# Start addresses of the on-chip tiles that TensorE reads, moved to multiples of 256 bytes

## The chip, the cores and the metric

The kernel runs on one core of a Trainium2 chip. The metric is device time in microseconds of one execution; the time given for a kernel is the median over runs. A core has a matrix engine (TensorE, PE in the profile, with its weight loads listed apart as PEld), three engines for elementwise work (VectorE = DVE, ScalarE = ACT, GpSimd = POOL), and SyncE (SP), which here only issues transfers. On-chip memory has 128 partitions; a tile takes the same range of bytes in each of them, and "address" below means the byte at which that range begins.

## What is computed

A decoder trunk of two layers over 1024 tokens with 1024 channels, batch 1, all in float32. Cut to what matters:

```python
def reference(x, ...):
    h = x
    for layer in range(2):
        n = rms_norm(h, norm1_g[layer])
        if layer % 2 == 0:
            mix = retention_rwkv_mixer(n, ...)   # 8 retention heads and 8 RWKV-7 heads, one output projection
        else:
            mix = swa_sink_mixer(n, ...)         # 16-head sliding-window attention (128) with sinks
        h = h + mix
        n = rms_norm(h, norm2_g[layer])
        h = h + (silu(n @ w_gate) * (n @ w_up)) @ w_down    # 2816 hidden channels
    return rms_norm(h, final_g)
```

## The kernel before

Activations are held transposed: channels on partitions, tokens along the tile, in two halves of 512 tokens. Every large product is made of matmuls with a 128x128 piece of weights held in the array (the stationary operand) and a 128x512 piece of activations streaming through it (the moving operand). To keep float32 accuracy with the faster fp32r format, each operand x is kept as a pair, hi = x rounded to fp32r and lo = x - hi, and each product is three matmuls: hi with hi, weights hi with activations lo, weights lo with activations hi. Those three are the lines 345 to 347 in `gemm`, 1168 to 1170 in `prod`, and three calls of line 239 (`mm`) in the first mixer's planner.

The order of stages, with the profile's times: the first mixer up to about 660 us (projections interleaved with many small float32 matmuls of the RWKV and retention heads; a planner with costs and due times written by hand sets that order); its output projection up to about 730; the FFN of layer 0 up to about 1345; attention up to about 1780; the FFN of layer 1 up to about 2340; the last norm. The FFNs use a two-by-two Strassen-like scheme with seven products instead of eight. `ffn_early` makes two of the products for each pair of hidden tiles; `late` (called by `ffn_pair`, eleven pairs a layer) makes the other five for the gate and the up matrix in step. Of these five, two have moving operands in `n8` tiles (`X["t2"]`, `X["t1"]`) and three in `cb` tiles (`X["t3"]`, `X["t4"]`, `X["22"]`). `down` and `rest_d` make the down projection, with moving operands in `n8` and `ha`.

Weights arrive by DMA in `wr`, `wq` or `wd` tiles and are split into hi and lo by ACT and by POOL or DVE into a tile of 128x1024 that holds 4 pieces of each (`wsplit`, lines 330 and 331; `vsplit`, lines 1341 and 1342). These tiles come from `wtile`: four buffers `w` in the pool `pp`, in some stages also the two `wr` buffers, and around attention two buffers `wx` in the pool `at`, one after the other in turn. `attn` projects with 12 weight tiles a half, `w_o` with 8.

Where tiles lie: a pool takes its memory from the left end or from the right end (`side`). Within a pool, tiles lie one behind the other in the order in which their tags first come. `t` rounds a tile up to a multiple of 16 words, 64 bytes. On the left stand 1024 bytes of scratch for DMA descriptors (line 1823), four small constants of 32 bytes each, and then `pp`, which stays open for the whole run: `pv` (98 words, rounded to 448 bytes), `c_ones` (512), `c_eps` (64), `wr`, `w`, `c_ident`, `n8`, `nq`. The pools opened later on the left (`rp`, `hx`, `nb`, `sp` of layer 1, `ft`, `wqa`, `wqb`, `fa`, `fz`) begin where `pp` ends. On the right stands a `pad` of 480 bytes, and the others stack down from it: `mx` (held as `mp`) and `mz` in the first mixer, later `hy`, `sp` of layer 0, `cb`, `nB`, `at`. Addresses in the first mixer, before the change:

```
pp:  pv 1152   c_ones 1600   c_eps 2112   wr 2176, 6272   w 10368 ...   c_ident 26752   n8 27264 ...
rp:  r2 68224 ...   c_cos, c_sin 84608, 86656   z 88704   c_dmask 90816   c_qdec 91840   rvm 92352   Sc 92416
mz:  rr 94272   rkk 98368   rv 102464   BK 107072
mp:  hv 119360   hk 119424   zlast 119488   Srw 119552   ...   id2 126848   gup 127104   ...   vm 219520   X 219648
```

When a pool is opened where another one stood, each new tile waits until the old tiles that it overlaps have been read for the last time (`reuse_waits="tile"`).

Every address used in this text is the one that the program's allocation gives for the named tile; the trace itself holds no addresses.

Of the kernel before, what the change touches and what calls it, by code (L numbers as in the profile page):

```python
# [10 lines left out]
F32 = mybir.dt.float32  # L11
# [5 lines left out]
P = 128  # L17
T = 1024
HT = 512
# [185 lines left out]
class Kern:  # L205
    def __init__(self, ctx, tc, A, out):
        self.ctx, self.tc, self.nc, self.A, self.out = ctx, tc, tc.nc, A, out
        nc = self.nc
        self.pp = ctx.enter_context(tc.tile_pool(name="pp", bufs=1, side="left"))
        self.dr = ctx.enter_context(tc.tile_pool(name="dr", bufs=2, space=bass.MemoryType.DRAM))  # L210
        self.n = 0
        pad = ctx.enter_context(tc.tile_pool(name="pad", bufs=1, side="right"))
        pt = pad.tile([P, 120], F32, tag="pad", name="pad")
        nc.gpsimd.memset(pt, 0.0)
        nc.scalar.activation(pt[:, :16], pt[:, :16], AF.Copy)
        self.pv = self.t(self.pp, [P, NPV], "pv")
        nc.scalar.dma_start(self.pv, A["pvec"])
        self.cst = {}
        for nm in ("ones", "eps"):
            self.cst[nm] = self.const(self.pp, nm)  # L220
        self.h, self.plan = [None, None], None
        self.wx = None
        self.w6, self.nw, self.owed, self.lo = False, 0, [], self.nc.gpsimd
        self.hid = [self.dram(f"hid{i}", [FT, P, HT]) for i in range(4)]
        self.hc = [self.dram(f"hc{L}", [NP, 4, P, 2, HT]) for L in range(2)]
        self.bd = self.dram("bd", [KT, P, HT])
        self.u0d = self.dram("u0", [NP, 2, P, HT])
        self.wsp = self.dr.tile([30, 2, P, 2, HT], F32, tag="wsp", name="wsp", bufs=1)
        self.cats = [self.dram(f"cat{hf}", [KT, P, HT]) for hf in range(2)]
# [37 lines left out]
    def t(self, pool, shape, tag, bufs=1, dt=F32):  # L267

        self.n += 1
        n = math.prod(shape[1:])  # L270
        if n % 16 == 0:
            return pool.tile(shape, dt, tag=tag, name=f"{tag}_{self.n}", bufs=bufs)
        t = pool.tile([shape[0], -(-n // 16) * 16], dt, tag=tag, name=f"{tag}_{self.n}", bufs=bufs)[:, :n]
        return t.rearrange("p (a b) -> p a b", b=shape[2]) if len(shape) == 3 else t

    def n8(self, pool):

        return [self.t(pool, [P, 2, HT], "n8", 8, F32R) for _ in range(8)]
# [112 lines left out]
    def mixer0(self):  # L391
        nc = self.nc
        gm, mp = self.pool("mx", "right")
        gz, self.mz = self.pool("mz", "right")
        gr, rp = self.pool("rp", "left")
        self.mp, self.rp = mp, rp
        hv = self.t(mp, [P, 12], "hv")
        nc.vector.tensor_scalar(
            out=hv[:, 0:8], in0=self.pv[:, PV["w0"] : PV["w0"] + 8], scalar1=0.5, scalar2=None, op0=ALU.mult
        )  # L400
        hk = self.t(mp, [P, 8], "hk")
        ka = self.pv[:, PV["ka"] : PV["ka"] + 4]
        nc.vector.tensor_scalar(out=hk[:, 0:4], in0=ka, scalar1=0.5, scalar2=None, op0=ALU.mult)
        nc.vector.tensor_scalar(out=hk[:, 4:8], in0=ka, scalar1=-0.5, scalar2=1.0, op0=ALU.mult, op1=ALU.add)
        self.hv, self.hk = hv, hk
        self.zlast = self.t(mp, [P, 14], "zlast")
        nc.gpsimd.memset(self.zlast, 0.0)
        self.Srw = self.t(mp, [P, 4, 64], "Srw")
        self.Sret = self.t(mp, [P, 4, 64], "Sret")
        self.wa, self.gl, self.cs, self.rs = None, None, None, None  # L410
        nc.gpsimd.memset(self.Srw, 0.0)
        nc.gpsimd.memset(self.Sret, 0.0)
        pl = self.plan = Plan(self)
        pq = self.psum("ps0", {"f": 3, "m": 4, "c": 1})
        self.pr, self.st, self.rst, self.dns, self.nds, self.last = {}, {}, {}, {}, {}, {}
        units = [(0, 0), (0, 2), (1, 0), (1, 2)]

        def jobs(hf, what, ps):
            for p in ps:
                if what == "rkv":  # L420
                    for i, nm in enumerate("rkv"):
                        self.shifted(hf, 4 * i + p, nm, p)
                else:
                    self.ret_jobs(hf, p)


        pl.chain(self.first_norm())
        for u, (hf, p0) in enumerate(units):
            pl.chain(self.unit(u, hf, (p0, p0 + 1)))
        for u, (hf, p0) in enumerate(units):  # L430
            for p in (p0, p0 + 1):
                pl.chain(self.pair(u, hf, p))
        for hf in range(2):
            for p in range(4):
                pl.chain(self.ret(hf, p))
        pl.chain(self.second_norm())
        self.lora(0)
        jobs(0, "rkv", (0, 1))
        jobs(0, "ret", (0, 1))
        jobs(0, "rkv", (2, 3))  # L440
        jobs(0, "ret", (2, 3))
        self.lora(1)
        jobs(1, "rkv", (0, 1))
        jobs(1, "ret", (0,))
        jobs(1, "rkv", (2, 3))
        jobs(1, "ret", (1, 2, 3))
        self.lo = nc.vector
        pl.run()
        self.lo = nc.gpsimd
        gr.__exit__(None, None, None)  # L450
        self.ghx, self.hx = self.pool("hx", "left")
        self.h[0] = self.wout(0, self.heads(0, self.n8(self.pp)), self.s8(self.hx, "h0", 2))
        gz.__exit__(None, None, None)
        gb, nb = self.pool("nb", "left")
        ch = self.heads(1, self.n8(nb), self.last)
        gm.__exit__(None, None, None)
        return pq, gb, nb, ch
# [27 lines left out]
    def loads(self):  # L485

        nc, mp, rp = self.nc, self.mp, self.rp
        x0 = []
        first = [self.plan.jobs[i] for i in range(4)]

        self.plan.twice = [j["col"] for j in first[:3]]
        for k in range(KT):
            x = self.t(rp, [P, HT], "r2", 8)
            self.keep(nc.sync.dma_start(x, self.A["xT"][k, :, 0:HT]))
            x0.append(x)
            if k == 0:
                raw = self.t(self.pp, [P, 1024], "wr", 2)
                for o in (0, HT):
                    self.keep(nc.sync.dma_start(raw[:, o : o + HT], self.A["w_in"][first[0]["col"]][:, o : o + HT]))
                first[0]["hl"] = self.wsplit(raw)  # L500
            if k == 4:
                raw = self.t(self.pp, [P, 1024], "wr", 2)
                self.keep(nc.sync.dma_start(raw, self.A["w_in"][first[1]["col"]]))
                first[1]["hl"] = self.wsplit(raw)
        for j in first[2:]:
            raw = j["raw"] = self.t(self.pp, [P, 1024], "wr", 2)
            self.keep(nc.sync.dma_start(raw, self.A["w_in"][j["col"]]))
        wua = self.t(mp, [P, 512], "wua")
        self.keep(nc.sync.dma_start(wua[0:64, :], self.A["w_up"]))
        self.keep(nc.sync.dma_start(wua[64:128, :], self.A["a_up"]))  # L510
        for nm in ("blk", "smask", "gmask", "ident", "kdec", "gam", "id2"):
            self.cst[nm] = self.const(self.pp if nm == "ident" else mp, nm, eng=nc.sync)
        gup = self.t(mp, [P, 512], "gup")
        nc.sync.dma_start(gup, self.A["g_up"])
        self.wua, self.gup = wua, gup
        return x0
# [99 lines left out]
    def shifted(self, hf, ti, nm, p):  # L616
# [3 lines left out]
        def evac(ps):  # L620
            tag = {"r": "rr", "k": "rkk", "v": "rv", "w": "wa", "g": "gl"}[nm]
            t = self.t(self.mz if nm in "rkv" else self.mp, [P, (64 if nm == "v" else 0) + HT], tag, 1 if nm == "w" else 2)
            out = t[:, 64:] if nm == "v" else t
            z = self.t(self.rp, [P, HT + 1], "z", 1)
            nc.gpsimd.tensor_copy(z[:, 0:1], self.zlast[:, ti : ti + 1])
            nc.vector.tensor_tensor(out=z[:, 1 : HT + 1], in0=ps, in1=self.rs, op=ALU.mult)
            nc.gpsimd.tensor_copy(self.zlast[:, ti : ti + 1], z[:, HT : HT + 1])
# [20 lines left out]
    def pair(self, u, hf, p):  # L648


        nc, mp = self.nc, self.mp
# [120 lines left out]
        for w in range(2):  # L772
            ps = self.pst("m", [P, 4, 2, 64])
            for j in range(4):
                o = 64 * (1 - w) + 128 * j
                self.tr(ps[:, j].rearrange("p e t -> p (e t)"), vp[:, o : o + 128], ident)
            mean = self.t(mp, [P, 4, 2], "vm", 2)
            V.tensor_reduce(out=mean, in_=ps, axis=AX.X, op=ALU.add, negate=True)

            if w == 0:  # L780
# [24 lines left out]
        for c in range(NCH):  # L805
            for e in range(2):
                b = half[1 - e]
# [211 lines left out]
    def ret(self, hf, p):  # L1019
        nc, mp = self.nc, self.rp  # L1020
# [18 lines left out]
        ps = self.pst("m", [P, 8, 64])  # L1039
        for c in range(4):  # L1040
            self.tr(ps[:, 2 * c : 2 * c + 2, :].rearrange("p e t -> p (e t)"), v[:, P * c : P * c + P], ident)
        mean = self.t(mp, [P, 8], "rvm", 1)
        V.tensor_reduce(out=mean, in_=ps, axis=AX.X, op=ALU.add, negate=True)
        vt = self.t(mp, [P, 4, 2, 64], "r2", 8)
        V.scalar_tensor_tensor(
# [788 lines left out]
```

## Time and profile before

| | us |
|---|---|
| median of 3 runs | 2386.26 (2385.11 to 2391.5) |
| span of the profiled execution | 2386.7 |
| PE busy, share of the span | 2323.7, 97% |
| weight loads (PEld), inside PE's time | 1829.0, 77% |
| DVE, ACT, POOL busy | 1669.3, 1053.3, 949.0 |
| mean granted TensorE clock | 0.990 of full |
| mean busy share of the 16 DMA engines | 0.49 |

The span is the time from the first to the last instruction of one profiled execution. Matmuls are pipelined: one starts while its predecessor is still draining, so the durations in the profile (390 ns and more for a 128x512 fp32r matmul) are longer than the spacing of the starts, and it is the spacing that adds up to the time. It is read from the timeline, which has a row per matmul in order of time, as the difference of two start times divided by the number of rows between them.

### The profile page before, as it was taken

To read this page: it belongs to the slowest core of one execution; us is meant where nothing else is said; L and a number is where in the kernel's file an instruction comes from. 1 tells how busy PE (TensorE), PEld (TensorE's weight loads), DVE (VectorE), ACT (ScalarE), POOL (GpSimd) and SP (SyncE) were. 2 spreads that over 40 slices of the span, in tenths; PEclk is the share of its full clock that TensorE was granted. 3 is DMA by queue.
4 is the path that set the end of the run, shared out by engine and by line. 5 is a ranking of instruction groups with operands and counts; after the bars stand their busy time and mean duration, and the time that the engine had idled before them with its cause. 6 is when DMAs were issued, how large, how long until landed. Compare 5 with 4: busy or idle time off the path is not lost. (4 is left out here: it accounts for less than half of the span.)

```text
span 2386.7 us, 35626 instructions
## 1 busy us (share of the span) xinstructions
PE 2323.7 (97%) x13092; PEld 1829.0 (77%) x13092; DVE 1669.3 (70%) x2630; ACT 1053.3 (44%) x1946; POOL 949.0 (40%) x746
## 2 busy tenths in 40 slices
PE   8999999999999999999999999999999999999997
PEld 6777677777777888887778877677788888887885
DVE  6876855774667358887675568567548778888776
ACT  5354433324456333333333556456645333333335
POOL 3122221201342057776567300002102677767665
PEclk9999999999999999999999999999999999999998
DMA  7655544443445545554554322231346555547652
GB/s 276 204 190 196 179 149 133 129 114 111 147 164 183 204 164 205 209 194 161 214 217 141 130 65 65 69 128 66 103 128 221 171 211 213 203 177 278 238 199 88
DMA packets 167741, 395.92 MB, mean 166 GB/s; under 512 B 42896, under 2 KB 45584, under 8 KB 167568
## 3 DMA queue, kind: packets, MB, share of 16 engines
q1 hardware_dynamic: 164448, 388.15, 47.6%
q10 hardware_dynamic: 2832, 4.45, 0.5%
q8 instruction: 104, 1.70, 0.3%
q0 software_dynamic: 288, 1.05, 0.1%
q14 instruction: 69, 0.57, 0.1%
HBM read 271.29 MB, written 116.92 MB: 163 GB/s over the span
## 5 line engine op out<-in xcount | busy, mean ns | idle before, releaser
L239 PE MATMUL ps_f<-n,w 128*128 128x512 f32 x1440 | 385.7, 415 | 11.1 <-ACT w L330 6.6
L239 PEld LDWEIGHTS ps_f<-n,w 128*128 128x128 f32 x1440 | 267.7, 192 | 96.5 <-issue 24.3
L330 ACT CAST w<-wr 128x512 fp32r<-128x512 f32 x244 | 147.8, 612 | 190.5 <-PE ps_f L347 76.0
L331 POOL TENSOR_TENSOR w<-wr,w 128x512 fp32r<-128x512 f32 x68 | 91.3, 1350 | 285.3 <-ACT w L330 227.1
L331 DVE TENSOR_TENSOR w<-wr,w 128x512 fp32r<-128x512 f32 (+1 forms) x176 | 124.1, 708 | 72.5 <-ACT w L330 72.0
L331 POOL TENSOR_TENSOR w<-wq,w 128x512 fp32r<-128x512 f32 x92 | 131.9, 1444 | 29.3 <-ACT w L330 27.2
L346 PE MATMUL ps_f<-n,w 128*128 128x512 f32 x356 | 142.8, 401 | 0.0
L345 PE MATMUL ps_f<-n,w 128*128 128x512 f32 x356 | 141.8, 398 | 1.0 <-ACT n L1594 0.5
L347 PE MATMUL ps_f<-n,w 128*128 128x512 f32 x356 | 142.0, 399 | 0.6 <-POOL w L331 0.6
L1175 DVE TENSOR_TENSOR nq<-ps_m,u 128x512 f32<-128x512 f32 x88 | 58.8, 685 | 107.1 <-PE ps_m L1170 106.9
L331 POOL TENSOR_TENSOR wx<-wr,wx 128x512 fp32r<-128x512 f32 x8 | 10.6, 1319 | 303.6 <-ACT wx L330 303.5
L1168 PE MATMUL ps_f<-n,w 128*128 128x512 f32 x298 | 119.2, 400 | 5.6 <-DVE h L1368 4.0
L1169 PE MATMUL ps_f<-n,w 128*128 128x512 f32 x298 | 117.8, 395 | 0.1
L1168 PE MATMUL ps_m<-n,w 128*128 128x512 f32 x300 | 117.0, 390 | 0.7 <-ACT w L1341 0.7
L1170 PE MATMUL ps_f<-n,w 128*128 128x512 f32 x298 | 117.5, 395 | 0.0
L1170 PE MATMUL ps_m<-n,w 128*128 128x512 f32 x300 | 117.1, 390 | 0.0
L1169 PE MATMUL ps_m<-n,w 128*128 128x512 f32 x300 | 117.1, 390 | 0.0
L1168 PE MATMUL ps_m<-cb,w 128*128 128x512 f32 x240 | 94.8, 395 | 0.9 <-DVE nq L1175 0.9
L353 POOL TENSOR_TENSOR n<-nq,n 128x512 fp32r<-128x512 f32 x54 | 91.5, 1709 | 9.3 <-ACT n L351 9.3
L1170 PE MATMUL ps_m<-cb,w 128*128 128x512 f32 x240 | 94.8, 395 | 0.0
L1169 PE MATMUL ps_m<-cb,w 128*128 128x512 f32 x240 | 94.7, 395 | 0.0
L1342 POOL TENSOR_TENSOR w<-wd,w 128x512 fp32r<-128x512 f32 (+1 forms) x53 | 75.3, 1430 | 33.3 <-ACT w L1341 33.3
(525 smaller groups left out, 6471.2 us busy)
## 6 DMA issues: line engine op xcount, KB each, us to landing
hc<-n SPq DMA_DIRECT2D x74, 512.0 KB, 2.8
wsp<-w SPq DMA_DIRECT2D x54, 512.0 KB, 3.6
w<-wsp SPq DMA_DIRECT2D x54, 512.0 KB, 3.6
wq<-in_w_gate SPq DMA_DIRECT2D x44, 512.0 KB, 4.3
u<-u SPq DMA_DIRECT2D x88, 256.0 KB, 2.9
n<-hc SPq DMA_DIRECT2D x43, 512.0 KB, 5.4
wr<-in_w_in SPq DMA_DIRECT2D x34, 512.0 KB, 4.9
hid<-n SPq DMA_DIRECT2D x66, 256.0 KB, 2.0
```

The lines of the kernel that those rows point to most:

```text
L239: self.nc.tensor.matmul(out, lhsT, rhs, **kw)
L330: nc.scalar.copy(hi[:, :n], raw[:, c])
L331: self.lo.tensor_tensor(out=lo[:, :n], in0=raw[:, c], in1=hi.bitcast(F32)[:, :n], op=ALU.subtract)
L345: nc.tensor.matmul(ps, hi, rh, start=k == 0, stop=False)
L346: nc.tensor.matmul(ps, hi, rl, start=False, stop=False)
L347: nc.tensor.matmul(ps, lo, rh, start=False, stop=k == n - 1)
L353: e.tensor_tensor(out=lo, in0=src, in1=hi.bitcast(F32), op=ALU.subtract)
L1168: mm(ps, hi, xh, start=first and k == 0, stop=False, skip_group_check=True)
L1169: mm(ps, hi, xl, start=False, stop=False, skip_group_check=True)
L1170: mm(ps, lo, xh, start=False, stop=last and k == len(w) - 1, skip_group_check=True)
L1175: add = lambda o, x, y: V.tensor_tensor(out=o, in0=x, in1=y, op=ALU.add)
L1342: nc.gpsimd.tensor_tensor(out=lo, in0=v, in1=hi.bitcast(F32), op=ALU.subtract)
```

## The change

No instruction is added, removed or changed. Three unused tiles (`gapt`) take up room, and three small tiles are made larger, with the program using the same part of them as before:

- a gap of 128 bytes ahead of `pv`, at the beginning of `pp`;
- a gap of 64 bytes at the beginning of `mp`, and one of 128 bytes ahead of `gup`;
- `z` takes 2304 bytes instead of 2112; each of the two `vm` 128 instead of 64; `rvm` 256 instead of 64.

```diff
@@ -213,6 +213,7 @@
         nc.scalar.activation(pt[:, :16], pt[:, :16], AF.Copy)
+        self.gapt(self.pp, 32)
         self.pv = self.t(self.pp, [P, NPV], "pv")
@@ -272,6 +273,10 @@
+    def gapt(self, pool, n):
+
+        pool.tile([P, n], F32, tag=f"gap{n}", name=f"gap{n}_{self.n}", bufs=1)
@@ -394,6 +399,7 @@
         self.mp, self.rp = mp, rp
+        self.gapt(mp, 16)
         hv = self.t(mp, [P, 12], "hv")
@@ -510,6 +516,7 @@
             self.cst[nm] = self.const(self.pp if nm == "ident" else mp, nm, eng=nc.sync)
+        self.gapt(mp, 32)
         gup = self.t(mp, [P, 512], "gup")
@@ -621,7 +628,7 @@
-            z = self.t(self.rp, [P, HT + 1], "z", 1)
+            z = self.t(self.rp, [P, HT + 64], "z", 1)[:, : HT + 1]
@@ -774,7 +781,7 @@
-            mean = self.t(mp, [P, 4, 2], "vm", 2)
+            mean = self.t(mp, [P, 32], "vm", 2)[:, :8].rearrange("p (a b) -> p a b", b=2)
@@ -1039,7 +1046,7 @@
-        mean = self.t(mp, [P, 8], "rvm", 1)
+        mean = self.t(mp, [P, 64], "rvm", 1)[:, :8]
```

## The prediction

> **What bounds the kernel now.** I read the page first, then the busy time by stage, then single matmuls in order of time.
>
> ```profile
> span 2386.7 us, 35626 instructions
> PE 2323.7 (97%) x13092; PEld 1829.0 (77%) x13092; DVE 1669.3 (70%) x2630; ACT 1053.3 (44%) x1946; POOL 949.0 (40%) x746
> ```
>
> TensorE (PE) is busy 97% of the span, and its weight loads (PEld) lie inside that time. The profiled execution's span, 2386.7, is 0.4 us above the median of the three runs, 2386.26; sums below are made against the span and then moved by that 0.4.
>
> ```profile
> core 0: us, PE busy (x) PEld busy (x) DVE busy (x) ACT busy (x) POOL busy (x), PEclk, DMA share, GB/s
> 60.00:660.00 600.00, 579.29 (x5298) 442.74 (x5297) 406.79 (x881) 252.10 (x409) 133.47 (x147) 0.98 0.49 154
> ...
> 840.00:1140.00 300.00, 299.12 (x1298) 243.30 (x1298) 228.26 (x249) 103.97 (x177) 206.77 (x144) 1.00 0.54 191
> ...
> 1320.00:1380.00 60.00, 60.00 (x265) 48.95 (x264) 35.06 (x48) 32.28 (x55) 18.24 (x17) 1.00 0.33 109
> 1380.00:1740.00 360.00, 355.77 (x1806) 263.67 (x1805) 248.17 (x561) 215.25 (x552) 26.37 (x21) 1.00 0.25 83
> 1740.00:1850.00 110.00, 110.00 (x476) 89.29 (x475) 74.91 (x104) 54.07 (x91) 22.74 (x15) 1.00 0.55 182
> 1850.00:2120.00 270.00, 270.00 (x1171) 219.21 (x1170) 216.54 (x240) 95.67 (x164) 191.34 (x133) 1.00 0.56 198
> ```
>
> In the second halves of the two FFNs (840 to 1140 and 1850 to 2120) and in the stages around attention PE has no idle time worth the name, at full clock, while DVE, the next engine, is busy 76 to 80%. There a matmul that starts its successor 6 ns sooner shortens the run by 6 ns. In the first mixer (60 to 660) PE idles 20.7 us and follows chains of small work. In 840 to 1140 PE's only wait is this one:
>
> ```profile
> PE ps_m L1168 <- DVE nq L1175: 0.9, 1, 0.9
> ```
>
> So the question is what one matmul costs from start to start, and whether that hangs on where its operands begin.
>
> **The natural experiment in the trace.** I went through the program in order and gave every matmul the start address of its moving operand and of the weights that load while it streams, those of the matmul behind it. Before the change nearly everything in the left-hand pools (`w`, `wr`, `n8` of `pp`, `ha`) begins at 128 modulo 256, and the right-hand pools opened after the mixer (`cb`, `n8` of `nB`, `wx`) begin at 0. The fp32r matmuls, 128x512 all, thus fall into four kinds. The timeline of one FFN pair, first and last rows of two stretches (start us, us, engine, line, out<-in; rows leave numbers out, so `n8` is `n`):
>
> ```profile
> 985.51 0.39 PE L1168 MATMUL ps_m<-n,wr 128*128 128x512 f32 x1
> ...
> 996.43 0.40 PE L1168 MATMUL ps_m<-cb,w 128*128 128x512 f32 x1
> ...
> 1013.23 0.39 PE L1168 MATMUL ps_m<-n,w 128*128 128x512 f32 x1
> ```
>
> From 985.51 to 996.43 run 2 products x 2 matrices x 4 k-tiles x 3 = 48 matmuls with `n8` moving, both operands at 128: 10.92 us, 227.5 ns each. From 996.43 to 1013.23 run 3 x 2 x 4 x 3 = 72 with `cb` moving (0) and weights at 128: 16.80 us, 233.3 ns each. The same pool of weights, the same stage, no gap. Is it `cb` that is slow, or the pair? Attention's projections answer, where the weights go round between `w` (128) and `wx` (0). First the half whose `n8` lies in `nB` (0):
>
> ```profile
> 1518.35 0.40 PE L347 MATMUL ps_f<-n,wx 128*128 128x512 f32 x1
> ...
> 1527.88 0.40 PE L347 MATMUL ps_f<-n,w 128*128 128x512 f32 x1
> ...
> 1533.33 0.40 PE L347 MATMUL ps_f<-n,wx 128*128 128x512 f32 x1
> ...
> 1544.49 0.40 PE L347 MATMUL ps_f<-n,w 128*128 128x512 f32 x1
> ```
>
> Each of these rows is the last before the weights change. Moving 0 against weights at 128: 41 starts from 1518.35 to 1527.88, 9.53 us, 232.4 ns; 48 from 1533.33 to 1544.49, 11.16 us, 232.5 ns. Between them `wx`, both at 0: 24 in 5.45 us, 227.1 ns. Then a stage in which the moving `n8` is that of `pp` (128):
>
> ```profile
> 1744.59 0.40 PE L347 MATMUL ps_f<-n,wx 128*128 128x512 f32 x1
> ...
> 1755.48 0.40 PE L347 MATMUL ps_f<-n,w 128*128 128x512 f32 x1
> ...
> 1761.07 0.40 PE L347 MATMUL ps_f<-n,wx 128*128 128x512 f32 x1
> ...
> 1771.97 0.40 PE L347 MATMUL ps_f<-n,w 128*128 128x512 f32 x1
> ```
>
> Here it is `wx` that is slow: 24 in 5.59 us, 232.9 ns, against 48 in 10.89 (226.9) and 48 in 10.90 (227.1) with `w`. So **alike** (0 with 0, 128 with 128) costs 227.1 ns on the mean of these four stretches, and **unlike** costs 232.4 to 233.3, whichever of the two is at 0. Neither address is bad by itself.
>
> **The change, part by part.** Addresses first. `pp` starts at byte 1152 (1024 of DMA scratch, four constants of 32); the gap of 32 words puts `pv` at 1280, `c_ones` at 1728, `c_eps` at 2240 and `wr` at 2304, which is 9 x 256. All that follows on the left moves by 128, to 0. `c_ones` alone does not: 64 becomes 192. `z` grows from 2112 to 2304 bytes, so what lies behind it in `rp` keeps to 0. On the right, 64 + 128 + 128 bytes more in `mp` (two gaps, two larger `vm`) move the bottom of `mp` from 119360 to 119040, which with the gaps puts `Srw`, `gup`, `AR`, `GG`, `XA` and `UV` at 0, and `mz` with it (`rr`, `rkk`, `rv`, `BK` from 64 to 0). `cb`, `wx`, `nB` stay at 0. Every fp32r pair becomes alike.
>
> The terms are counts of unlike pairs, in program order, by the difference of such stretches.
>
> ```profile
> core 0: us, PE busy (x), PEclk, DMA share, GB/s
> ...
> 840.00:1160.00 320.00, 186.51 (x792) 1.00 0.55 193
> ...
> 1850.00:2150.00 300.00, 186.50 (x792) 1.00 0.55 195
> ```
>
> These are the matmuls with `cb`, 792 in each FFN: 1584 x (233.3 - 227.1) = 9.8 us, in stages where PE is full, so all of it counts.
>
> ```profile
> 1320.00:1380.00 60.00, 5.65 (x24) 1.00 0.33 109
> 1380.00:1740.00 360.00, 89.10 (x352) 1.00 0.25 83
> 1740.00:1850.00 110.00, 16.29 (x68) 1.00 0.55 182
> ```
>
> These are the matmuls with `wx`. In 1320 to 1380 all 24 are alike, and 80 with `w` are unlike; in 1740 to 1850, 56 with `wx` and 276 with `w` are unlike. PE is full in both: 356 x 5.4 = 1.9 us and 56 x 5.8 = 0.3 us. In attention (1380 to 1740) 400 with `w` and 136 with `wx` are unlike: 400 x 5.4 + 136 x 5.8 = 2.9 us. There the softmax chains on DVE and ACT could hold PE to their own pace, which would leave 0; PE is busy 355.77 of 360, nearer to full, so I take 2.0 between 0 and 2.9.
>
> The plain fp32 work of the mixer changes its pairs as well:
>
> ```profile
> L239 PE MATMUL ps_m<-rt,c_blk 128*128 128x512 f32 x32 | 16.8, 605 | 0.0
> L239 PE MATMUL ps_m<-GG 64*64 64x128 f32 x256 | 16.7, 273 | 0.7 <-DVE AR L926 0.7
> L239 PE MATMUL ps_m<-XA,GT 64*64 64x128 f32 x256 | 16.1, 273 | 1.4 <-ACT r L1035 0.9 <-DVE rt L681 0.5
> L239 PE MATMUL ps_m<-gl,gup 128*128 128x512 f32 x16 | 8.1, 598 | 0.0
> ```
>
> The small ones cost 273 ns alike (`GG` with `GG`) and unlike (`XA`, `GT`). Of the wide ones the unlike (`rt`, `c_blk`) shows 605, the alike (`gl`, `gup`) 598: about 100 such passes x 7 ns is 0.7 us at most, in a stage where PE waits on others anyway; I take 0, with 0.7 as the other end. `c_ones` has 12 matmuls and stays unlike either way. The gaps hold no data, and the larger `z` and `vm` are read in the same shape: 0. DMA rows now start at 0 as well; PE waits for no transfer in the full stages, so 0 there.
>
> Sum: 9.8 + 1.9 + 0.3 + 2.0 = 14.0 us off 2386.7 gives 2372.7 in the profile's terms, **2372.3** against the median. Ends: with the quickest alike stretch (226.9), all of attention and the 0.7, 10.1 + 2.0 + 0.3 + 3.1 + 0.7 = 16.2 us.
>
> **The rivals.**
> - *No effect.* The extra 6 ns belong to certain tiles (their pool, who writes them), and moving everything by 128 leaves each its cost: 2386. For it: all of `cb` is slow. Against it: the same `n8` of `nB` runs at 232.4 and at 227.1 within 10 us, and its two sets of weights are made by the same lines. The Trainium skill takes this side ("TensorE: Matmul & The Clock Gate", Step-by-step: what each phase is for: "Loading the next tile's weights doesn't steal SBUF read bandwidth from the running matmul"; "SBUF — State Buffer", Who interferes with whom, has PE wait on nobody). By these rules the address of the weights could not matter; the three stretches around 1530 us speak against them. Chance 6%.
> - *Half of it comes back as waits.* PE runs into the weight splits. For it: POOL is busy 69 and 71% and DVE 76 and 80% of the full stages, in bursts. Against it: PE waits 0.9 us there now, and the gain is 2 to 3% of these pairs. About 7 us kept: 2379.3. Chance 9%.
> - *Slower: a start at 0 is itself the slow one for the operand that streams.* For it: most matmuls with the moving operand at 0 are slow today (`cb`, 1584, and `nB` with `w`, 756). Then 5100 `n8` and 672 `ha` matmuls go from 128 to 0, about 5580 of them from alike, and each pays 6 ns: +33 us, 2420. It decides as soon as more than the 2500 unlike pairs are hit. Against it: the 24 with `wx` at 227.1 have the moving operand at 0. Chance 3%. A further 3% goes to moved tiles that wait for other former users of their memory; to end slower by 0.3% that must cost 21 us, as much as PE's whole idle time in the mixer.
>
> **How the numbers follow.** Forecast 79%, half 9%, none 6%, slower 6%. 0.3% of 2386 is 7.2 us, about what a measurement of this kernel tells from no change. The forecast's own ends, 11 to 16 us of gain, and 1 us of run-to-run spread give 2369 to 2377; the range goes up to the half case with the same spread, 2381, which leaves about 17% out. Faster takes the forecast and half of the half case, 0.83; same the other half and the case of none, 0.11; slower 0.06.
>
> **What would show each step.** In the new profile the stretches with `cb` should read 72 starts in about 16.35 us, as long per matmul as those with `n8` around them; `w` and `wx` in attention should not differ; PE busy in the two FFN halves should end about 5 us earlier each, with as many matmuls. The mixer up to 840 should keep its length within 2 us. I am wrong if `cb` stays at 233 (no effect), if `n8` with `w` at 660 to 840 rises above 230 (the absolute rule), or if PE gains waits of several us on ACT, DVE or POOL in 840 to 1140.

## The result, and the profile after

| kernel | runs | median, us | ratio to the kernel before |
|---|---|---|---|
| before | 6 | 2387.54 (2385.11 to 2391.50) | |
| changed | 6 | 2374.60 (2368.86 to 2381.18) | 0.9944 (0.9929 to 0.9958) |
| changed, measured again (e1) | 6 | 2378.30 (2372.31 to 2380.67) | 0.9957 (0.9943 to 0.9970), beside 2389.05 |
| changed, a third time (e11) | 6 | 2377.32 (2370.36 to 2378.27) | 0.9956 (0.9944 to 0.9969), beside 2386.50 |

The change makes the kernel 0.4 to 0.6% faster, 9 to 13 us between the medians (e1 and e11 had runs of the kernel before of their own, with the medians named in the last column). 2372.3 was forecast; the 18 runs of the changed kernel have a mean of 2376.0. The profiled execution of the changed kernel has a span of 2373.0 and a time of 2374.81. The order of instructions is the same on every engine, so each matmul can be held against itself. In the profile after, `prod` stands at lines 1175 to 1177, the three matmuls of `gemm` at 350 to 352, the late add at 1182, the column sums of the weights at 1208 to 1211 and `up` at 1226; before, they are 1168 to 1170, 345 to 347, 1175, 1201 to 1204 and 1219.

From the page of the changed kernel:

```profile
span 2373.0 us, 35626 instructions
PE 2312.1 (97%) x13092; PEld 1828.9 (77%) x13092; DVE 1667.4 (70%) x2630; ACT 1054.7 (44%) x1946; POOL 948.4 (40%) x746
```

PE's busy time fell by 11.6 us and its share stayed 97%; the busy times of the others moved by 2 us or less. The same stretches as in the prediction (us, then busy time and count for PE, PEld, DVE, ACT, POOL, then the granted clock, DMA share, GB/s):

```profile
core 0: us, PE busy (x) PEld busy (x) DVE busy (x) ACT busy (x) POOL busy (x), PEclk, DMA share, GB/s
60.00:660.00 600.00, 582.50 (x5328) 445.40 (x5327) 409.74 (x885) 253.43 (x411) 133.17 (x149) 0.98 0.48 155
840.00:1140.00 300.00, 299.03 (x1313) 245.59 (x1312) 230.03 (x253) 103.86 (x175) 203.60 (x141) 1.00 0.55 194
...
1380.00:1740.00 360.00, 355.77 (x1813) 265.23 (x1812) 252.23 (x568) 216.99 (x554) 25.94 (x20) 1.00 0.25 84
1740.00:1850.00 110.00, 107.69 (x465) 87.98 (x464) 72.00 (x100) 52.06 (x88) 28.10 (x19) 0.98 0.56 187
1850.00:2120.00 270.00, 270.00 (x1186) 221.80 (x1185) 221.71 (x239) 99.02 (x169) 198.50 (x138) 1.00 0.55 196
```

In 840 to 1140 PE now puts 1313 matmuls where it put 1298, and in 1850 to 2120 1186 where it put 1171. But in 1740 to 1850 it idles 2.31 us where it had no idle time, and the clock there is 0.98. Part of the gain was spent again, and this is the place. First the gain itself, in the timeline of the same matmuls as in the prediction:

```profile
979.69 0.39 PE L1175 MATMUL ps_m<-n,wr 128*128 128x512 f32 x1
...
990.76 0.39 PE L1175 MATMUL ps_m<-cb,w 128*128 128x512 f32 x1
...
1007.08 0.39 PE L1175 MATMUL ps_m<-n,w 128*128 128x512 f32 x1
...
1507.53 0.39 PE L352 MATMUL ps_f<-n,wx 128*128 128x512 f32 x1
...
1516.82 0.39 PE L352 MATMUL ps_f<-n,w 128*128 128x512 f32 x1
...
1522.26 0.39 PE L352 MATMUL ps_f<-n,wx 128*128 128x512 f32 x1
...
1533.14 0.39 PE L352 MATMUL ps_f<-n,w 128*128 128x512 f32 x1
```

The 72 starts with `cb` take 16.32 us, 226.7 ns each, where they took 233.3. In attention 41 starts take 9.29 us (226.6 ns, before 232.4), the 24 with `wx` 5.44 (226.7, before 227.1) and 48 more 10.88 (226.7, before 232.5): `w` and `wx` no longer differ. The 48 with `n8` ahead of `cb` need 11.07 us where they needed 10.92, and this pair is worth holding on to: none of them became slower by itself, but one hand-over among them did (below).

PE waits in the late FFN pairs of both layers, by engine and line waited for (total us, times, longest us), of the changed kernel; the first row is from 840 to 1140, the second from 1740 to 1850:

```profile
PE ps_m L1175 <- DVE nq L1182: 1.0, 1, 1.0
```

```profile
PE ps_m L1175 <- DVE sg L1226: 2.1, 1, 2.1
```

The first was there before (0.9). The second is new, and nothing like it stands in the profile of before.

For a balance by stage I took, for the first matmul of each stage, its start in each profile less its start in the profile of before, and the differences of these. Negative is time gained, in us; the predicted column is the prediction's terms put into the stages where their pairs lie (so many `cb` pairs at 6.2 ns, so many `n8` pairs at 5.4 or 5.8).

| stage (us in the profile of before) | predicted | after | e1 | e11 |
|---|---|---|---|---|
| start to 840 | 0 | -3.9 | -0.3 | +1.1 |
| 840 to 1140, late pairs of layer 0 | -4.6 | -3.5 | -3.5 | -3.5 |
| 1140 to 1320, end of these pairs, down projection | -0.3 | -2.5 | -1.3 | -4.7 |
| 1320 to 1380 | -0.4 | -0.5 | -0.5 | -0.5 |
| 1380 to 1740, attention | -2.0 | -2.0 | -2.0 | -0.6 |
| 1740 to 1850 | -1.8 | -1.5 | -1.6 | -2.0 |
| 1850 to 2120, late pairs of layer 1 | -4.5 | +0.2 | +0.2 | +0.2 |
| 2120 to the end | -0.4 | +0.1 | -0.6 | -0.5 |
| sum | -14.0 | -13.4 | -9.6 | -10.4 |

Two rows repeat to a tenth and are not what was predicted: 840 to 1140, and 1850 to 2120. Three rows vary by several microseconds between executions of one and the same program: up to 840, the down projection, attention. So that the first profile came within a microsecond of 14.0 owes something to luck: its 3.9 us up to 840 didn't come back in e1 or e11.

Much of what varies is the granted clock, which stands at half in stretches of 3.4 or 6.8 us; such a stretch costs half its length. In the down projection the profile of before and that of e1 have one of 6.8 us, the profile after has one of 3.4, and e11 has none. The later run e10, whose addresses are those of the kernel before, has none either, and gains 3.9 us in that row: the row says as much on the one profile of before as on the change.

### The profile page after: what moved, and what is told of

Read it like the earlier page. It is cut to its first block, busy times and chain, and to the rows that moved or that the text cites. A ratio compares the mean times of both kernels' runs of the same rounds, so it can differ in the third digit from the quotient of the medians.

```text
span 2373.0 us, 35626 instructions
## 1 busy us (share of the span) xinstructions
PE 2312.1 (97%) x13092; PEld 1828.9 (77%) x13092; DVE 1667.4 (70%) x2630; ACT 1054.7 (44%) x1946; POOL 948.4 (40%) x746
```

## The experiments

### Which addresses matter

Two kernels make the fp32r pairs alike in other ways than the change. The first has only one of its edits, the gap at the beginning of `pp`; the mixer's right-hand pools stay where they were (`z`, `vm`, `rvm` too). The second moves nothing on the left, and everything on the right by 128, so that the pairs are alike at 128 where the change has them at 0.

```diff
# e2, against the kernel before (gapt as in the change)
+        self.gapt(self.pp, 32)
         self.pv = self.t(self.pp, [P, NPV], "pv")
```

```diff
# e3, against the kernel before
-        pt = pad.tile([P, 120], F32, tag="pad", name="pad")
+        pt = pad.tile([P, 152], F32, tag="pad", name="pad")
```

> The changed kernel once more, in more rounds and with a second profile. Theory (the cost belongs to the pair: moving operand and the weights that load meanwhile, alike or 128 apart modulo 256): ratio 0.994, cb from start to start 226.7 ns again. The first profile of the changed kernel also shows a new wait of 2.1 us on DVE near 1837 us (sg L1226) and fewer half-speed stretches of the TensorE clock in the mixer. If these two belong to the change, they come again; rival: they are of one execution, and the second profile shows a gain before 840 us of less than 2 us instead of 3.9, and the half-speed stretches at other places.

> Only the first gap, ahead of pv: every fp32r pair is alike at 0, while the mixer's float32 tiles on the right stay at 128 or 64 (GG, AR, XA, UV, gup, rr, BK) and now stand apart from what lies on the left. Theory: the fp32r pairs are all of the gain; ratio 0.994, within 3 us of the changed kernel. Rival (the mixer's own edits bring the 3.9 us that the changed profile gained before 840 us): 2378 to 2380, ratio 0.996 to 0.997.

> No gap on the left; the pad on the right is 128 bytes larger, so cb, wx and the n8 of nB go from 0 to 128 and every fp32r operand begins at 128. Theory of the pair: as quick as the changed kernel, ratio 0.994, cb at 226.7 ns. Rival (it is the multiple of 256 that is quick, for TensorE's reads or for the DMA rows that start there): no gain, 2387, or a loss.

Measured: e1 2378.30, ratio 0.9957; e2 2375.21 (2370.25 to 2381.36), 0.9950 (0.9935 to 0.9965); e3 2379.31 (2375.12 to 2382.28), 0.9963 (0.9951 to 0.9976). The three shared the runs of the kernel before, and their intervals overlap. In all three the 1584 matmuls with `cb` take 226.7 ns from start to start. The other edits of the change (the two gaps in `mp`, the larger `z`, `vm` and `rvm`) can't be told from nothing, and a multiple of 256 is no better a start than one 128 behind it. What counts is that the two operands agree. That they agree modulo 256 is enough: by the program's allocation, the alike pairs of the changed kernel lie a multiple of 512 apart (4041 of those behind 660 us that follow closely) or 256 more than that (2516), and both kinds cost 227.1 ns on the mean.

The fourth kernel turns this round. It puts the moving tiles at 0 and leaves the weights `w` and `wr` at 128: some 5300 pairs that were alike become unlike, and most of the 2500 unlike ones stay so.

```diff
# e4, against the kernel before: in first_norm, ahead of the first n8
+        self.gapt(self.pp, 32)
```

> A gap of 128 bytes between the weight tiles w, wr (which stay at 128) and n8: n8, ha and cb all at 0, so about 7,780 of the 8,364 fp32r pairs are 128 apart, 5,240 more than before. Theory of the pair: n with w goes from 227 to 232 to 233 ns in every stage; +5.4 to 6.2 ns each is +28 to +33 us, 2416 to 2420, ratio 1.012 to 1.014; 3 or 4 us less where the mixer waits on other engines. Rival (the two operands are read through ports of their own and do not meet; cb and nB are slow for another reason): no change, 2387.

Measured: 2402.64 (2398.58 to 2408.16), ratio 1.0064 (1.0048 to 1.0079), span 2401.6. The timeline, same matmuls as above:

```profile
993.02 0.39 PE L1173 MATMUL ps_m<-n,wr 128*128 128x512 f32 x1
...
1004.23 0.39 PE L1173 MATMUL ps_m<-cb,w 128*128 128x512 f32 x1
...
1021.02 0.39 PE L1173 MATMUL ps_m<-n,w 128*128 128x512 f32 x1
```

Now the 48 with `n8` take 11.21 us, 233.5 ns, like the 72 with `cb` at 16.79, 233.2. Slower it is, and by the mechanism, but by half of what was expected. Summed over all matmuls, the dearer ones cost about 25 us; 15 arrived at the end. From 60 to 660 the dearer matmuls add 3.3 us and PE's stalls shrink by 2.4; from 1220 to 1320 they add 2.0 and the stalls shrink by 6.1. A slower matmul fills time in which PE would have waited anyway. The price itself was smaller there too: 3.2 ns on the mean for the dearer matmuls of 60 to 660 that follow each other closely, 5.5 to 5.8 in the full stages of the FFNs. The prediction's rule, that each nanosecond counts, is a rule for full stages only.

### How far apart is apart

The same filler tile, in three other lengths, puts `cb`, `wx` and one of the `n8` at 192, 224 and 160 behind a multiple of 256, with the weights `w` and `wr` at 128.

```diff
# e6; e7 has 128 and e8 has 144 in place of 136
-        pt = pad.tile([P, 120], F32, tag="pad", name="pad")
+        pt = pad.tile([P, 136], F32, tag="pad", name="pad")
```

> The kernel before with its leading filler 16 words longer: cb and the n8 that was at 0 begin at 192 past a multiple of 256, w and wr at 128, so the unlike pairs are 64 bytes apart where before they were 128 apart. If any difference costs the whole, cb with w takes 232 to 234 ns start to start, as before. If it is the half of the 256 bytes that counts (both operands in the upper half are alike), 226 to 227.5 ns. If the cost grows with the distance, about 229 to 230.5 ns. The same for n8 with w. n8 with w where both begin at 128 stays at 226 to 228 ns under all three.

> The kernel before with its leading filler 8 words longer: cb and the one n8 begin at 224, w and wr at 128, 96 bytes apart. If any difference costs the whole, cb with w takes 232 to 234 ns start to start. If the half of the 256 bytes counts, 226 to 227.5. If the cost grows with the distance, about 231 to 232.

> The kernel before with its leading filler 24 words longer: cb and the one n8 begin at 160, w and wr at 128, 32 bytes apart. If any difference costs the whole, cb with w takes 232 to 234 ns start to start. If the half of the 256 bytes counts, 226 to 227.5. If the cost grows with the distance, about 228 to 229.

The 72 starts with `cb` of the prediction's pair, in e6, then a stretch of e6 with `wx` at 192 loading beside an `n8` at 128; then both stretches in e7 (`wx` at 224), then in e8 (`wx` at 160):

```profile
996.29 0.40 PE L1168 MATMUL ps_m<-cb,w 128*128 128x512 f32 x1
...
1012.79 0.40 PE L1168 MATMUL ps_m<-n,w 128*128 128x512 f32 x1
...
1753.27 0.39 PE L347 MATMUL ps_f<-n,w 128*128 128x512 f32 x1
...
1758.87 0.39 PE L347 MATMUL ps_f<-n,wx 128*128 128x512 f32 x1
```

```profile
995.57 0.40 PE L1168 MATMUL ps_m<-cb,w 128*128 128x512 f32 x1
...
1012.38 0.40 PE L1168 MATMUL ps_m<-n,w 128*128 128x512 f32 x1
...
1751.46 0.39 PE L347 MATMUL ps_f<-n,w 128*128 128x512 f32 x1
...
1757.07 0.39 PE L347 MATMUL ps_f<-n,wx 128*128 128x512 f32 x1
```

```profile
998.38 0.40 PE L1168 MATMUL ps_m<-cb,w 128*128 128x512 f32 x1
...
1015.18 0.40 PE L1168 MATMUL ps_m<-n,w 128*128 128x512 f32 x1
...
1758.47 0.40 PE L347 MATMUL ps_f<-n,w 128*128 128x512 f32 x1
...
1764.07 0.40 PE L347 MATMUL ps_f<-n,wx 128*128 128x512 f32 x1
```

| start of the moving operand less that of the weights, modulo 256 | ns from start to start | from |
|---|---|---|
| 0 | 226.7 | `cb` after |
| +32 (160, 128) | 233.3 (16.80 us / 72) | `cb` in e8 |
| +64 (192, 128) | 229.2 (16.50 / 72) | `cb` in e6 |
| +96 (224, 128) | 233.5 (16.81 / 72) | `cb` in e7 |
| 128 (0, 128) | 233.3 | `cb` before |
| -32 (128, 160) | 233.3 (5.60 / 24) | `n8` with `wx` in e8 |
| -64 (128, 192) | 233.3 (5.60 / 24) | `n8` with `wx` in e6 |
| -96 (128, 224) | 233.8 (5.61 / 24) | `n8` with `wx` in e7 |

"The half of the 256 bytes counts" falls: 160 and 224 lie in the same half as 128 and pay in full. "It grows with the distance" falls as well: 32 costs as much as 128. "Any difference costs the whole" holds but for one: with the moving operand 64 ahead of the weights the price is 2.5 ns and not 6.6, and with it 64 behind it is 6.6 again. Why that one is cheap is open, and so is whether it is the 64 or the start at 192 that does it, as no other run has a moving operand 64 ahead. The times, 2384.71, 2386.66 and 2393.32, are single runs, beside 2390.45 (2386.03 to 2393.47) for the kernel before; they lie as far apart as runs of one kernel do, and the verdict rests on the timeline.

### Where the rest of the gain went

The new wait, first as it was before. The timeline of the kernel before, all engines, around the first late pair of layer 1 (the bracket: idle time before the row, and what ended it):

```profile
1848.43 1.60 DVE L1202 TENSOR_TENSOR n<-n,n 128x512 f32<-128x512 f32 x1
...
1849.96 0.68 DVE L1219 TENSOR_TENSOR sg<-sg,ps_m 128x512 f32<-128x512 f32 x1
...
1850.68 0.19 PEld L1168 LDWEIGHTS ps_m<-n,wr 128*128 128x128 f32 x1 [0.19 <-DVE sg L1219]
1850.76 0.43 PE L1168 MATMUL ps_m<-n,wr 128*128 128x512 f32 x1
```

DVE's multiplication `sg<-sg,ps_m` reads the last early product out of an accumulator bank `ps_m`, and the late pair's matmul is the next to write that bank. DVE works its queue in order, and ahead of the multiplication stands a run of column sums of weights (lines 1201 to 1204; the first row is the last one ahead of it). It ended at 1850.64, and PE's weight load came at 1850.68: just in time. The same place in the changed kernel:

```profile
1836.98 1.59 DVE L1209 TENSOR_TENSOR n<-n,n 128x512 f32<-128x512 f32 x1
1838.50 0.67 DVE L1226 TENSOR_TENSOR sg<-sg,ps_m 128x512 f32<-128x512 f32 x1
...
1839.22 0.71 PE L1175 MATMUL ps_m<-n,wr 128*128 128x512 f32 x1 [2.07 <-DVE sg L1226]
...
1840.16 0.63 PE L1177 MATMUL ps_m<-n,wr 128*128 128x512 f32 x1
1840.58 0.63 PE L1175 MATMUL ps_m<-n,wr 128*128 128x512 f32 x1
```

PE is there earlier, DVE is not: its sums are no quicker. PE stands 2.07 us, and then runs at 427 ns a matmul (1840.16 to 1840.58) instead of 227. The windows show why, in the column of the granted clock:

```profile
1835.00:1840.00 5.00, 2.93 (x12) 2.15 (x11) 4.91 (x6) 0.62 (x1) 4.71 (x3) 0.93 0.04 14
1840.00:1845.00 5.00, 5.00 (x17) 3.94 (x17) 1.75 (x3) 1.14 (x2) 0.44 (x1) 0.72 0.77 262
```

DVE is busy 4.91 of 5 us while PE waits, and after the pause the clock stands at half for 3.4 us: the next nine matmuls take 3.76 us (1839.22 to 1842.98) where nine at 226.7 ns take 2.04, 1.7 more. The wait stands at 2.0 to 2.1 us in after, e1, e2 and e11 and 1.7 in e3, and neither in the kernel before nor in e4, where PE comes no earlier. The half-speed stretch followed in after, e1 and e11 and did not in e2 and e3: there 1850 to 2120 gains 1.4 and 1.7 us, and not the 0.2 lost of the table.

A second, smaller return comes once in each late pair. The changed kernel, all engines, at the beginning of a pair, where the first product of the gate matrix ends and that of the up matrix begins:

```profile
926.89 0.68 DVE L1182 TENSOR_TENSOR u<-ps_m,u 128x512 f32<-128x512 f32 x1
...
927.42 0.39 PE L1177 MATMUL ps_m<-n,w 128*128 128x512 f32 x1
...
927.68 0.19 PEld L1175 LDWEIGHTS ps_m<-n,wr 128*128 128x128 f32 x1 [0.30 <-issue]
927.71 0.47 PE L1175 MATMUL ps_m<-n,wr 128*128 128x512 f32 x1
...
928.02 0.40 PE L1176 MATMUL ps_m<-n,wr 128*128 128x512 f32 x1
```

Starts are 0.29 and 0.31 us apart where they are otherwise 0.227, 0.15 us in all. The bank that the up matrix writes next was read by DVE until 927.57 (the first row), behind another run of column sums, and the load of the weights, which otherwise begins with the matmul before it (927.42), came 0.11 us after that. There are eight such hand-overs in each layer, and at all sixteen the load begins 0.11 to 0.12 us after the end of this read. Eight make the 1.2 us by which 840 to 1140 stays behind its matmuls: those with `cb` alone gained 4.76 us there.

If this is right, another accumulator bank at these places gives the time back. e5 lets the last early pair of layer 1 use `ps_y`, which is idle then.

```diff
# e5, against the changed kernel
-                K.ffn_early(L, p, sp, "ff" if L and p < 6 else "fm")
+                K.ffn_early(L, p, sp, "ff" if L and p < 6 else "fy" if L and p == NP - 1 else "fm")
```

> The changed kernel with one more edit: the last early FFN pair of layer 1 accumulates in the ps_y bank where it took ps_m, so the first late pair finds ps_m free. In the changed kernel that late pair's first matmul waited about 2 us at 1840 for DVE's read of ps_m (the sg operation, queued on DVE behind the column sums of the weights). Theory (that wait is a give-back by itself): the wait on DVE sg at about 1840 is gone, the stretch 1740 to 1850 shrinks by 2 us more, and the time is 1.5 to 4 us under the changed kernel's, 2372 to 2374, a ratio of 0.993 to 0.9945 to the kernel before. Rival (DVE's burst of column sums is what PE runs into): the wait moves to another tile that DVE releases in the same 15 us, and the stretch stays as it was in the changed kernel within 0.5 us.

Measured: 2372.83 (2370.54 to 2374.78), ratio 0.9928 (0.9914 to 0.9942). Its timeline:

```profile
1842.39 0.67 DVE L1226 TENSOR_TENSOR sg<-sg,ps_y 128x512 f32<-128x512 f32 x1
...
1843.81 0.47 PE L1175 MATMUL ps_m<-cb,w 128*128 128x512 f32 x1 [0.42 <-DVE nq L1182]
```

The 2 us are gone; PE stops only at the next operation behind the same sums, for 0.42, and the clock stays whole. By matmul, 1740 to 1850 gained 2.0 (changed kernel 1.5) and 1850 to 2120 gained 2.8 (changed kernel: 0.2 lost). In sum that is 3.5 us, about the size of the wait and the slow clock behind it; it came in the second of the two stages, where the first had been named, since the late pair that waited starts behind 1850 in the profile of before. A small remainder of the rival is left. Of all kernels run this has the lowest median, and of those run several times the narrowest spread; it was not timed against the changed kernel on the same chip, and its interval overlaps that of the first measurement and lies just below the other two.

The other kernels let the late pairs use `ps_f` and `ps_m` in turn: e9 on the changed kernel, e10 on the kernel before, e12 on the changed kernel and in layer 1 alone.

```diff
# e9 and e10; e12 has "fm"[p % 2] if L else "m"
-            gens.append(self.late(self.pst("m", [P, HT]), self.pst("rc"[i], [P, HT]), next_w, u0s[i], u[i]))
+            gens.append(self.late(self.pst("fm"[p % 2], [P, HT]), self.pst("rc"[i], [P, HT]), next_w, u0s[i], u[i]))
```

> The changed kernel with one more edit: the late FFN pairs take their first two accumulators in turn from the ps_f and the ps_m banks, where every pair took ps_m. Theory (in the late pairs PE, now faster, runs into DVE's last read of ps_m, which stands behind a 1.66 us column sum on DVE): the one matmul of each pair that took some 306 ns is back at 227, the wait of 2 us on DVE sg at about 1840 is gone, the two stretches of late pairs each shorten by 1.0 to 1.3 us beside the changed kernel, and by matmul the end comes 3 to 5 us earlier than without the edit; time 2369 to 2373, ratio to the kernel before 0.991 to 0.993. Rival (PE runs into the split of the weights on ACT and POOL, which this edit doesn't touch): the 306 ns matmuls stay, and only the wait at 1840 may go.

> The kernel before with the same edit of the banks and no tile moved. By the theory PE there comes to ps_m after DVE has read it, so the edit is worth nothing: the late pairs and the end as in the kernel before, ratio 0.999 to 1.001. By the rival that the banks are a gain of their own, whatever the addresses: 2 to 4 us, ratio 0.998 to 0.9985.

> The changed kernel as it is, beside the two others on the same chip: 2373 to 2379, ratio 0.994 to 0.996, with the wait on DVE sg at about 1840 and the 306 ns matmuls in it; against it the edit of the banks is read.

> The changed kernel with ps_f and ps_m in turn for the late pairs of layer 1 alone (layer 0 as in the changed kernel, where the edit left the first stretch of late pairs as long as it was). Theory (what the edit is worth lies in layer 1, where it takes away the wait on DVE sg at about 1840): beside the kernel before, by matmul, the stretch 840 to 1140 is 3.4 to 3.5 us shorter as in the changed kernel and 1850 to 2120 is 3.6 to 4.0 us shorter, where the changed kernel had 0.2 longer to 0.2 longer; time 2370 to 2374, ratio 0.992 to 0.994. Rival (waits that leave one bank come back at another): 1850 to 2120 shortens by less than 2.5 us.

Measured: e9 2373.92 (2371.83 to 2379.26), 0.9950 (0.9937 to 0.9964), beside e11 with 0.9956; e10 2387.63 (2384.69 to 2391.74), 1.0002 (0.9993 to 1.0010); e12 2376.82 (2372.99 to 2380.42), 0.9946 (0.9931 to 0.9961). e9 and e12 fall short of the ratios that were expected (0.991 to 0.993, 0.992 to 0.994): their times can't be told from the changed kernel's. e10 settles one point: in the kernel before, the banks are worth nothing. They become a limit only when PE is quicker.

On the hand-overs the theory was wrong in part. Groups of matmuls from 1850 to 2120 (count, then shortest, median and longest in ns), the changed kernel and then e12:

```profile
L1175 PE MATMUL ps_m<-n,w x56: 387/389/470, 1860.2 to 2111.2; 128*128 128x512 f32 x56
...
L1175 PE MATMUL ps_m<-n,wr x24: 387/389/468, 1887.4 to 2084.0; 128*128 128x512 f32 x24
...
L1175 PE MATMUL ps_m<-cb,w x99: 389/389/389, 1850.0 to 2097.6; 128*128 128x512 f32 x99
```

```profile
L1175 PE MATMUL ps_m<-n,w x28: 388/390/390, 1853.7 to 2085.0; 128*128 128x512 f32 x28
```

```profile
L1175 PE MATMUL ps_m<-cb,w x56: 388/389/469, 1878.2 to 2101.8; 128*128 128x512 f32 x56
```

The late matmul of 470 ns has left the first product of the pair (with `n8`) and stands in the third (with `cb`), the next to write a bank that DVE has to read first. There are about as many as without the edit, at about 0.08 us each where they cost 0.15. With the banks in turn one wait for DVE has become another wait for DVE, and 840 to 1140 gains 3.3 in e9 where it gained 3.5 without. What the edit is worth lies in layer 1, in the wait at 1840: 1850 to 2120 gains 3.8 us in e9 and 3.6 in e12, against 0.2 lost. The totals don't show it as clearly as the stage does: in e12's profile attention is 1.1 us longer than before (the clock is at half there twice, for 3.4 us each), and in e9 the first matmul of the down projection waits for a weight split it had not waited for. The profiled executions of e9 and e10 also spend 2.7 to 2.8 us outside the span where all others spend 1.8; the cause of this is open.

## Why the prediction was right, and where its sizes were off

- **Alike and unlike.** Right, and shown from three sides: made alike at 0 (the change), made alike at 128 (e3), made unlike (e4). By the Trainium skill's sentence that loading weights "doesn't steal SBUF read bandwidth from the running matmul" ("TensorE: Matmul & The Clock Gate", Step-by-step: what each phase is for) the start of the weights would not matter; the trace does not bear this out for operands that start apart, 233.3 ns against 226.7. The rival of no effect is out.
- **The 1584 pairs with `cb`, 9.8 us.** The matmuls gained 10.3 us, as all alike pairs settled at 226.7, 0.4 under the 227.1 taken. What failed is the half-sentence behind it, "so all of it counts": the late pairs kept 3.5 us in layer 0 and lost 0.2 in layer 1.
- **`n8` of `nB` outside attention, 2.2 us.** The matmuls gained 2.3.
- **Attention, 2.0 between 0 and 2.9.** 2.0 in two profiles and 0.6 in the third, which has a half-speed stretch there. The unlike pairs fell by 3.7 ns on the mean and not by 5.4. The long unbroken stretches fell by 5.8 (the 41 and the 48 above); in stretches of 5 to 20 matmuls between other products most fell by 0 to 4, and no run shows why. So choosing between the ends was right, and the reason given for it, that the softmax chains set the pace, stays unshown.
- **The mixer, 0.** -3.9, -0.3 and +1.1 up to 840. No steady gain, and "within 2 us" was missed by the first profile, by the luck of one execution. The sign named against the absolute rule stayed away: from 660 to 840 the fp32r matmuls that follow closely cost 227.0 ns after and 226.9 before.
- **The rival of waits.** It was given a tenth and half of the gain. It happened: of the 14.4 us that the matmuls gained, 6.2 came back in the two stages of late pairs in after, e1 and e11 (1.2 and 5.0). That the medians still end 9 to 13 us lower goes with the rows of the balance that vary between executions. It came in another place than the prediction looked. Not the weight splits on POOL and ACT, but DVE's read of an accumulator bank behind a run of column sums, at the first late pair of layer 1: 2.07 us, 1.7 more by the half-speed stretch behind them, and 0.15 at the hand-over in each pair. In 840 to 1140, where the prediction asked to look, PE's waits stayed at 1.0. The profile of before did show it: the row at 1850.68, released by DVE 0.04 us earlier. A wait of 0.19 us reads like nothing, and says that PE has no lead left there.
- **The rival on the other side.** A start at 0 is not slow (the changed kernel is all at 0), but what it would have cost can be read from e4, which made nearly as many pairs dearer (5300 for 5580): 2402.6, and not 2420, as the price was smaller in part and stages with waits take up some of it.
- **The range.** Its lower end is not worked out in the sum: with attention at 0 the terms give 12.0 us, and the 11 of the range stands beside it without a row. And 1 us of run-to-run spread was too little: single runs of the changed kernel lie up to 12 us apart, and its three medians 3.7.

So the forecast of 14.0 us was right in its mechanism and in the raw size. The medians lie 2 to 6 us above its time; it took every microsecond in a full stage as kept, and the late pairs gave 6.2 back.

## What to carry to other kernels

Where fp32r matmuls follow each other closely with a weight load in each, place the moving operand and the weights so that they start alike modulo 256; which start it is doesn't matter (0 and 128 cost the same here). Read the gain from start to start in the timeline, matmul against the same matmul, and look for places with little or no lead in the profile of before (a wait of 0.1 or 0.2 us, a release just before the load), since that is where a quicker engine will stand next. Then give the accumulator that is read behind a burst of other work a bank of its own. The Trainium skill asks that independent groups of matmuls rotate through different PSUM banks ("Perfetto Trace Analysis", Matmuls). e5 agrees with it at one place, and e9, with two banks in turn in all late pairs, shows that the waits of the hand-overs only move to the next turn of a bank.

## What the runs showed of the hardware

- A 128x512 fp32r matmul that streams while the next weights load costs 226.7 ns if both start alike modulo 256, and 233 to 234 ns if they are 32, 96 or 128 apart, either way. At +64 it costs 229.2, at -64 233.3.
- After pauses of PE the granted clock can stand at half, in stretches of 3.4 or 6.8 us (the last of an execution is longer), during which a matmul takes 427 ns. In the 3.4 us ahead of each such stretch, in all fourteen profiles, PE had idled for 0.4 us or more. The same wait of 2.0 to 2.1 us was followed by such a stretch in three profiles and not in a fourth. These stretches come to 44 to 61 us in each profile, and where they fall differs between executions of one program; with them the stages up to 840, the down projection and attention vary by 1.4 to 5 us.
- In the changed kernel, a weight load that waits for DVE's read of its bank begins 0.11 to 0.12 us after that read ends, and costs 0.15 us: 0.29 and 0.31 us between starts in place of 0.227 twice. In e12 it costs 0.08, and in the kernel before, at 1850.68, 0.04. In the rows of the changed kernel the load begins 0.03 us ahead of its own matmul, where it otherwise begins with the matmul before it.
